# An encoder layer in fp32r halves on one core: conv tiles ahead of v, and the input stage's mean and three roots from column sums on whole tiles

## The chip, the cores and the metric

One core of a Trainium2 chip runs the whole layer. The metric is the device time of one execution in microseconds; it is the median of three runs.

## The reference

One layer of a hybrid encoder, batch 1, 512 tokens (a grid of 8 rows by 64), width 2048, fp32. What matters of it:

```python
xn = rms_norm(x, attn_norm_g[l])
proj = xn @ w_in[l]                          # 2048 -> 5120
u_val, u_gate, q, k, v = split(proj)         # 1024 columns each
h = depthwise_conv(u_val * sigmoid(u_gate), dw_w, dw_b)      # width 31
y_conv = silu(layer_norm(h, ln_g, ln_b))     # over the 1024 channels
y_na = neighborhood_attention(q, k, v, rpb)  # 16 heads of 64, window 8 x 16
mixed = concat(rms_norm(y_conv, conv_out_g), rms_norm(y_na, na_out_g))
x = x + mixed @ w_out[l]                     # 2048 -> 2048
...                                          # norm, gated MLP (5632) with a conv of width 3, norm
```

So the input stage has, over the channels of each token, one mean and one root for the LayerNorm (named `rln`), one root for the conv group's norm (`ra`) and one for the attention group's (`rna`).

## The kernel before

Activations lie transposed: channels on the 128 partitions, 512 tokens along the free axis, so a tile is 128x512. An fp32 product is made of three fp32r products: every weight chunk is loaded raw (SP queue), ScalarE copies it to fp32r (`whi`, L129) and VectorE forms the rest (`wlo`, L130). There are four buffers of each, and `weights()` makes three chunks ahead of the one in use. Nine raw buffers are shared with the conv tiles' accumulators `y` and the attention's bias tables. A *unit* below is one chunk of weights against eight chunks of the input: 16 matmuls with `whi` (L146 and L147) and 8 with `wlo` (L149).

`ORDER` (L63) writes the tiles of the input projection out by hand: `a` is a pair of conv tiles (gate and value, four units), `V` half of v (eight chunks, L396), `q` one attention pair's q and k (four units). Each `a` puts the 31 taps of its depthwise conv into a list; each chunk that is made takes up to `TAPS` = 4 of them, which run on VectorE (L462, L464). The order of VectorE's and ScalarE's queues is chosen by the framework's scheduler when the program is built, from priorities and from "issue after" marks; each engine then runs its queue in order.

Other work hangs on `tick`, which is called behind every unit and moves two generators on by one step, first the attention, then `group_a`:

- The attention takes a pair of heads at a time (pairs 0 to 7): behind one tick come the values of the pair before (L585, `po`) and this pair's scores (L539, `sc`), then the softmax (VectorE L549 to L555, ScalarE L554 and L557). Three ticks later, or four for the pairs in `LATER` = (5, 6), the probabilities are turned on TensorE (L565, `trp`) and copied by ScalarE (L574, `pt`). The values of that pair follow one tick after.
- `group_a` starts when all taps are done: sum of the eight conv tiles (L477, L479), column sums of it on TensorE (L482), the mean (L484), subtraction and squares (L487, L220, L221), the root `rln`, then for each tile the product with it (L494), silu (L495), the split into `mah` and `mal` (L211, L212), squares again (L220, L221), and after `RA_AFTER` ticks the root `ra`.

A root is made in `rsqrt_steps` and `root_steps`: four fp32 matmuls with one column each (L261, eight rows of the trace) bring the sums of squares onto the tokens' partitions; seven operations on 128x4 form the inverse root; it is spread on two diagonal tiles `dg` (eight products of 128x128, L248); one tick later two matmuls with ones (L252) broadcast it to all partitions, and ScalarE copies it (L254). PSUM banks of the projections (`psm`) are three in rotation; `stat()` has one bank that it shares with the values.

The output projection's first half (`out_half(ma, read_a)`, L146 to L149 with names `po` and `mah`) runs while the last attention pairs are still under way; `read_a` holds its results in their banks until `ra` is there (L673, L674). The second half, and the MLP behind it (L800, L939), are not touched.

Of the kernel before, what the change touches and what calls it, by code (L numbers as in the profile page):

```python
# [10 lines left out]
F32 = mybir.dt.float32  # L11
F32R = mybir.dt.float32r
AF = mybir.ActivationFunctionType
ALU = mybir.AluOpType
AX = mybir.AxisListType

P = 128
# [3 lines left out]
CONV = 1024  # L21
HEADS = 16
DH = 64
NA = 1024
# [4 lines left out]
EPS = 1e-6  # L29
# [5 lines left out]
U = 8  # L35
# [18 lines left out]
TAPS = 4  # L54
# [5 lines left out]
Q = D // 2 // S  # L60
TAIL = 4
ROW = 2048
ORDER = "aaaaaVVqaqaqaqqqqq"  # L63
LATER = (5, 6)
RA_AFTER = 5

# [11 lines left out]
def layer(ctx: ExitStack, tc: tile.TileContext, xT, xg, xn, xw, w_0, w_in, w_v, w_out, w_up, w_down, par, tab, g3, out):  # L78
    nc = tc.nc
# [8 lines left out]
    @contextmanager  # L88
    def shifted(by):

        at = tc.cur_priority
        tc.cur_priority = max(at + by, 0)
        yield
        tc.cur_priority = at + (tc.cur_priority - max(at + by, 0))

    def t2(name, dt=F32):
        return tp.tile([P, S], dt, tag="t2k", name=name)

    def t4(shape, name):

        return wpool.tile(shape, F32, tag="raw", name=name, bufs=NR)
# [4 lines left out]
    def pc(name, i):  # L106
        o = POFF[name] + i
        return prm[:, o:o + 1]

    ones_r = consts.tile([P, P], F32R, name="ones")  # L110
    ones = ones_r.bitcast(F32)
# [3 lines left out]
    ps = psm.tile([P, S], F32, tag="mm", name="warm")  # L115
# [5 lines left out]
    def raw_unit(src, n):  # L121
        raw = t4([P, U * P], "raw")
        return raw, nc.sync.dma_start(raw[:, :n], src)

    def parts(raw, n):
        hi = wpool.tile([P, U * P], F32R, tag="whi", name="whi", bufs=NW)
        lo = wpool.tile([P, U * P], F32R, tag="wlo", name="wlo", bufs=NW)
        with tc.issue_after(copies.pop().ins) if copies else nullcontext():
            i = nc.scalar.activation(hi[:, :n], raw[:, :n], AF.Copy)  # L129
        j = nc.vector.tensor_sub(lo[:, :n], raw[:, :n], hi[:, :n].bitcast(F32))  # L130
        with tc.issue_after(j.ins), shifted(600):
            for _ in range(min(len(taps), TAPS)):
                taps.pop(0)()
        return hi, lo, i, j

    def unit(src, n):

        return parts(raw_unit(src, n)[0], n)[:2]

    tight, taps, copies = [], [], []  # L140

# [26 lines left out]
    plan, made = [], []  # L168
# [39 lines left out]
    def split(src, g, name):  # L208

        h, l = t2(name + "h", F32R), t2(name + "l", F32R)  # L210
        nc.scalar.activation(h, src, AF.Copy, scale=g)  # L211
        nc.vector.scalar_tensor_tensor(l, src, g, h.bitcast(F32), op0=ALU.mult, op1=ALU.subtract)  # L212
        return h, l

    def sum_sq(acc, src, first, to=slice(0, S)):
        if first:
            nc.scalar.activation(acc, src, AF.Square)
        else:
            q = t2("sq")[:, to]
            nc.scalar.activation(q, src, AF.Square)  # L220
            nc.vector.tensor_add(acc, acc, q)  # L221

    def stat():
        if where:
            return psa.tile([P, S], F32, tag="tr", name="st", bufs=2)
        return psa.tile([P, S], F32, tag="po", name="st")
# [3 lines left out]
    def root_steps(sums, n, name, keep=None):  # L230

        v, r, y = (sm.tile([P, S // P], F32, tag="rs" + c, name="rs" + c) for c in "vry")
        h = sm.tile([P, S // P], F32R, tag="rsh", name="rsh")
        nc.vector.tensor_scalar(v, sums, 1.0 / n, EPS, op0=ALU.mult, op1=ALU.add)
        nc.scalar.activation(r, v, AF.Sqrt)
        nc.vector.tensor_mul(y, r, r)
        nc.vector.tensor_add(y, y, v)
        nc.vector.reciprocal(y, y)
        nc.vector.scalar_tensor_tensor(y, y, 2.0, r, op0=ALU.mult, op1=ALU.mult)
        nc.vector.tensor_copy(h, y)  # L240
        nc.vector.tensor_sub(v, y, h.bitcast(F32))
        if keep is not None:
            nc.vector.tensor_copy(keep, y)

        dg = [t2("dg", F32R) for _ in range(2)]
        for d, x in zip(dg, (h.bitcast(F32), v)):
            for i in range(S // P):
                nc.vector.tensor_scalar(d[:, i * P:(i + 1) * P], ident, x[:, i:i + 1], None, op0=ALU.mult)  # L248
        yield
        ps = stat()  # L250
        for i in range(2):
            nc.tensor.matmul(ps, ones_r, dg[i], start=i == 0, stop=i == 1)  # L252
        res = t2(name)
        nc.scalar.activation(res, ps, AF.Copy)  # L254
        return res

    def rsqrt_steps(acc, n, name):

        ps = stat()
        for i in range(S // P):  # L260
            nc.tensor.matmul(ps[:, i:i + 1], acc[:, i * P:(i + 1) * P], ones[:, 0:1], start=True, stop=True)  # L261
        return (yield from root_steps(ps[:, :S // P], n, name))


    xs, x1 = [], []
    pin = tc.keep_in_program_order

# [7 lines left out]
    def piece(k0, k1):  # L275
        n = 3 * (k1 - k0) * P
        raw, i = raw_unit(w_0[:, 3 * k0 * P:3 * k1 * P], n)
        pin(i)
        w = parts(raw, n)
        for i in w[2:]:  # L280
            pin(i)
        pieces.append((k0, k1, [w[0]], w[1]))
# [10 lines left out]
    for k in range(ROWS):  # L293
        n = 3 * P
# [3 lines left out]
        x, raw, lo = both[:, :S], both[:, S:S + n], t2("wel", F32R)[:, :n]  # L298
# [4 lines left out]
        else:  # L303
            his = [t2("weh", F32R)[:, :P], t2("weh", F32R)[:, P:n]]
            h, l = t2("xh", F32R), t2("xl", F32R)
# [22 lines left out]
    for u in range(2):  # L328
        raw, i = raw_unit(w_in[1, :, u * U * P:(u + 1) * U * P], U * P)
# [5 lines left out]
    for i in range(6):  # L335
        plan.append(lambda i=i: parts(early[i - 4], U * P)[:2] if i > 3 else None)
    a_, q_, v_ = iter(range(NC_)), iter(range(NP_)), iter(range(2))
    for step in ORDER:
        if step == "V":
            half = next(v_)  # L340
            for u in range(KD // 2):
                plan.append(lambda half=half, u=u: unit(w_v[half, u], U * P))
            continue
        i = next(a_ if step == "a" else q_)
        for n in ((NC_ + i, i) if step == "a" else (2 * NC_ + j * NP_ + i for j in range(2))):
            for u in range(KD // U):
                plan.append(lambda n=n, u=u: unit(w_in[n, :, u * U * P:(u + 1) * U * P], U * P))
    del plan[6:14]
    for half in range(2):
        for d in range(KD):  # L350
            plan.append(lambda half=half, d=d: unit(w_out[half, d], U * P))
# [118 lines left out]
    ma, ra = [], []  # L470

    def group_a():
        yield
        while taps:
            yield
        acc = t2("acc")
        nc.vector.tensor_add(acc, ys[0], ys[1])  # L477
        for i in range(2, NC_):
            nc.vector.tensor_add(acc, acc, ys[i])  # L479
        yield  # L480
        ps = stat()
        nc.tensor.matmul(ps, ones, acc, start=True, stop=True)  # L482
        mu = t2("mu")
        nc.vector.tensor_scalar(mu, ps, 1.0 / CONV, None, op0=ALU.mult)  # L484
        acc = t2("acc")
        for i in range(NC_):
            nc.vector.tensor_sub(ys[i], ys[i], mu)  # L487
            sum_sq(acc, ys[i], i == 0)
        yield
        yield  # L490
        r = yield from rsqrt_steps(acc, CONV, "rln")
        acc = t2("acc")
        for i in range(NC_):
            nc.vector.tensor_mul(ys[i], ys[i], r)  # L494
            nc.scalar.activation(ys[i], ys[i], AF.Silu, scale=pc("lng", i), bias=pc("lnb", i))  # L495
            ma.append(split(ys[i], pc("cog", i), "ma"))
        for i in range(NC_):
            sum_sq(acc, ys[i], i == 0)
        for _ in range(RA_AFTER):
            yield  # L500

        ra.append((yield from rsqrt_steps(acc, CONV, "ra")))


    mb, rb = [], []
    acc_na = t2("accna")
# [119 lines left out]
    p, n = -1, 0  # L626
    for step in ORDER:
        if step == "a":
# [34 lines left out]
    wait = []  # L663

    def norm_b():
        rb.append((yield from rsqrt_steps(acc_na, NA, "rna")))

    def read_a(d, ps):
        wait.append((d, ps))
        while ra and wait:  # L670
# [3 lines left out]
            nc.vector.tensor_add(x2[d], x2[d], t)  # L674

    steps.append(norm_b())
    assert len(ma) == NC_
    out_half(ma, read_a)
# [328 lines left out]
    def all_but_one(th, t):  # L1007

        m = sm.tile([P, 1], F32, tag="nm", name="rsm")
        nc.vector.tensor_reduce(m, sq[th][:, t, :2 * Q - 1], axis=AX.X, op=ALU.add)  # L1010
        nc.vector.tensor_scalar(m, m, 1.0 / D, EPS, op0=ALU.mult, op1=ALU.add)
        return m
# [52 lines left out]
    for i in product2(5, primed, True):  # L1065
        with shifted(-100):
            for _ in ready(e3, primed, 0, 0, (i,), True, fused):
                pass
            if i % Q == Q - 2:
                most = all_but_one(0, i // Q)  # L1070
# [78 lines left out]
```

## Time and profile before

| | |
|---|---|
| median of three runs | 1961.36 us (1961.08 to 1961.88) |
| profiled execution | 1961.11 us, its span 1959.3 us |
| TensorE busy | 1944.6 us |
| VectorE busy | 1607.2 us |
| ScalarE busy | 1083.0 us |
| mean granted TensorE clock | 0.997 |

Times in the profile are from one execution. TensorE matmuls are pipelined, so rows overlap the next; a row's idle time is in brackets, with what ended it. L numbers are lines of the kernel before; where a line of the changed kernel is meant, the text says so.

### The profile page before, as it was taken

To read this page: it belongs to the slowest core of one execution; us is meant where nothing else is said; L and a number is where in the kernel's file an instruction comes from. 1 tells how busy PE (TensorE), PEld (TensorE's weight loads), DVE (VectorE), ACT (ScalarE), POOL (GpSimd) and SP (SyncE) were. 2 spreads that over 40 slices of the span, in tenths; PEclk is the share of its full clock that TensorE was granted. 3 is DMA by queue.
4 is the path that set the end of the run, shared out by engine and by line. 5 is a ranking of instruction groups with operands and counts; after the bars stand their busy time and mean duration, and the time that the engine had idled before them with its cause. 6 is when DMAs were issued, how large, how long until landed. Compare 5 with 4: busy or idle time off the path is not lost.

```text
span 1959.3 us, 28088 instructions
## 1 busy us (share of the span) xinstructions
PE 1944.6 (99%) x10359; PEld 1655.9 (85%) x10359; DVE 1607.2 (82%) x2345; ACT 1083.0 (55%) x1721; POOL 225.4 (12%) x310
## 2 busy tenths in 40 slices
PE   9999999999999999999999999999999999999998
PEld 8888888878788888888888888888888888888886
DVE  5987888887558898888888888888889898885764
ACT  7222344458526666666666666666666644554654
POOL 0111111100011111111111111111110300000000
PEclk9999999999999999999999999999999999999999
DMA  9676767767758899999999999999995966666653
GB/s 372 180 195 178 203 179 189 184 175 225 239 157 211 207 261 242 273 245 267 243 268 248 267 249 263 254 257 260 251 260 165 389 234 236 216 216 193 192 201 121
DMA packets 141530, 448.90 MB, mean 229 GB/s; under 512 B 14928, under 2 KB 27216, under 8 KB 139984
## 3 DMA queue, kind: packets, MB, share of 16 engines
q1 hardware_dynamic: 89168, 291.90, 43.2%
q0 software_dynamic: 42624, 148.92, 34.9%
q10 hardware_dynamic: 9600, 6.29, 1.1%
q8 instruction: 81, 1.33, 0.3%
q14 instruction: 57, 0.47, 0.1%
HBM read 428.17 MB, written 111.15 MB: 275 GB/s over the span
## 4 chain that ended last, share of the span: by engine, by line
PE 95%; DVE 2%; ACT 2%; issue 1%; DMA 0%; DVEq 0%
PE pu L800 44%; PE pd L939 21%; PE pj L146 5%; PE pj L147 5%; PE pj L149 4%; PE pv L396 4%; PE po L149 3%; PE po L146 3%; PE po L147 3%; PE pj L434 1%; PE pj L438 1%; DVE wlo L130 1%; DVE acc L221 0%; PE po L585 0%; PE trp L565 0%
## 5 line engine op out<-in xcount | busy, mean ns | idle before, releaser
L129 ACT ACTIVATE whi<-raw 128x1024 fp32r<-128x1024 f32 (+1 forms) x574 | 604.3, 1055 | 566.5 <-PE pj L147 118.1
L130 DVE TENSOR_TENSOR wlo<-raw,whi 128x1024 fp32r<-128x1024 f32 (+1 forms) x574 | 698.9, 1219 | 215.6 <-ACT whi L129 178.0
L800 PE MATMUL pu<-xc,whi 128*128 128x512 f32 x2464 | 593.6, 391 | 0.0
L800 PEld LDWEIGHTS pu<-xc,whi 128*128 128x128 f32 x2464 | 451.3, 188 | 86.7 <-DVE xc L688 0.4
L800 PEld LDWEIGHTS pu<-xc,wlo 128*128 128x128 f32 x2464 | 319.2, 191 | 13.7
L800 PE MATMUL pu<-xc,wlo 128*128 128x256 f32 x2464 | 324.2, 283 | 0.0
L939 PE MATMUL pd<-whi,ho 128*128 128x512 f32 x1232 | 305.1, 389 | 0.1
L939 PEld LDWEIGHTS pd<-whi,ho 128*128 128x128 f32 x1232 | 231.1, 188 | 48.7 <-DVE vl L813 0.5
L146 PE MATMUL pj<-xh,whi 128*128 128x512 f32 x464 | 183.8, 396 | 0.0
L464 DVE SCALAR_TENSOR_TENSOR y<-ch,prm,y 128x500 f32<-128x500 f32 (+14 forms) x240 | 177.4, 742 | 5.8
L147 PE MATMUL pj<-xl,whi 128*128 128x512 f32 x464 | 181.7, 392 | 0.0
L939 PE MATMUL pd<-wlo,ho 128*128 128x512 f32 x616 | 165.1, 389 | 0.0
L939 PEld LDWEIGHTS pd<-wlo,ho 128*128 128x128 f32 x616 | 115.6, 188 | 24.0
L809 ACT ACTIVATE pu<-pu 128x512 f32<-128x512 f32 x132 | 76.5, 580 | 92.9 <-PE pu L800 92.8
L749 POOL DMA_DIRECT2D raw<-in_w_up x88 | 78.1, 887 | 354.8 <-DVE wlo L130 195.5
L203 POOL DMA_DIRECT2D ws<-in_w_down x88 | 79.4, 902 | 309.0 <-DMA ws<-in_w_down 114.1
L149 PE MATMUL pj<-xh,wlo 128*128 128x512 f32 x464 | 114.7, 389 | 0.0
L146 PEld LDWEIGHTS pj<-xh,whi 128*128 128x128 f32 x464 | 88.0, 190 | 19.9 <-issue 1.9
L147 PEld LDWEIGHTS pj<-xl,whi 128*128 128x128 f32 x464 | 87.9, 189 | 18.1 <-issue 0.2
L149 PEld LDWEIGHTS pj<-xh,wlo 128*128 128x128 f32 x464 | 87.1, 188 | 18.1
L200 POOL DMA_DIRECT2D ws<-ws x44 | 23.1, 526 | 310.7 <-PE pu L800 84.1
L200 POOL DMA_DIRECT2D ws<-in_w_down x44 | 23.2, 528 | 308.5 <-PE pj L149 127.2
(203 smaller groups left out, 2110.2 us busy)
## 6 DMA issues: line engine op xcount, KB each, us to landing
raw<-in_w_up SPq DMA_DIRECT2D x220, 512.0 KB, 5.9
ws<-in_w_down POOLq DMA_DIRECT2D x132, 512.0 KB, 6.1
raw<-in_w_up POOLq DMA_DIRECT2D x88, 512.0 KB, 7.5
raw<-ws SPq DMA_DIRECT2D x88, 512.0 KB, 3.6
raw<-in_w_down SPq DMA_DIRECT2D x66, 512.0 KB, 4.4
raw<-in_w_in SPq DMA_DIRECT2D x58, 512.0 KB, 5.4
ws<-ws POOLq DMA_DIRECT2D x44, 512.0 KB, 5.8
raw<-in_w_out SPq DMA_DIRECT2D x32, 512.0 KB, 5.6
```

What stands on the lines that cost most here:

```text
L129: i = nc.scalar.activation(hi[:, :n], raw[:, :n], AF.Copy)
L130: j = nc.vector.tensor_sub(lo[:, :n], raw[:, :n], hi[:, :n].bitcast(F32))
L146: nc.tensor.matmul(ps, hi, mh, start=first and k == 0, stop=False)
L147: nc.tensor.matmul(ps, hi, ml, start=False, stop=False)
L149: i = nc.tensor.matmul(ps, lo[:, wk * P:(wk + 1) * P], mh, start=False, stop=last and k == len(ws) - 1)
L203: nc.gpsimd.dma_start(wsum[c][k], w_down[k, {1: A21, 2: A11, 4: A11, 6: A12}[c]], accum_op=ALU.add, max_dma_last_dim=ROW)
L396: m = nc.tensor.matmul(banks[c], xs[2 * u + k][x][:, c * P:(c + 1) * P], w[l][:, k * S:(k + 1) * S], start=u == x == l == k == 0, stop=las ...
L464: nc.vector.scalar_tensor_tensor(y[:, a:b], h[:, a + j - PAD:b + j - PAD], prm[:, o:o + 1], y[:, a:b], op0=ALU.mult, op1=ALU.add)
L749: nc.gpsimd.dma_start(a[c], w_up[f, q2], accum_op=ALU.add)
L800: i = nc.tensor.matmul(ps[:, :n], part[:, k * P:(k + 1) * P], comb[c][k][:, :n], start=j == 0 and not more, stop=j == 2 * U - 1, skip_grou ...
L809: nc.scalar.activation(to, ps, AF.Copy)
L939: m = nc.tensor.matmul(ps[i], h[:, o + t * P:o + (t + 1) * P], w[:, d], start=start and not more and kind == 0 and j == 0, stop=stop and k ...
```

## The change

The order of tiles has six conv pairs ahead of v instead of five, the seventh and eighth come before and after the first q, and the other seven q follow without a break. While v is made, five taps are taken per chunk instead of four. The column sums for the mean are made of two fp32r halves instead of fp32. The three roots `rln`, `ra` and `rna` no longer go over 128x4 and diagonals: the sums of squares are split in two halves, two matmuls with ones give the column sums on all partitions at once, and the inverse root is formed there on 128x512 tiles. In `group_a` the number of ticks between the steps changes with it. The first root (`rstd1`) and the MLP's (`rstd2`) stay as they were.

```diff
-ORDER = "aaaaaVVqaqaqaqqqqq"
+ORDER = "aaaaaaVVaqaqqqqqqq"
...
-    def parts(raw, n):
+    def parts(raw, n, most=TAPS):
...
-            for _ in range(min(len(taps), TAPS)):
+            for _ in range(min(len(taps), most)):
                 taps.pop(0)()
...
+    def halved(src):
+
+        h, l = t2("ah", F32R), t2("al", F32R)
+        nc.scalar.activation(h, src, AF.Copy)
+        nc.vector.tensor_sub(l, src, h.bitcast(F32))
+        return h, l
+
+    def column_sums(two):
+
+        ps = stat()
+        for i in range(2):
+            nc.tensor.matmul(ps, ones_r, two[i], start=i == 0, stop=i == 1)
+        return ps
+
+    def roots_of_sums(acc, n, name, wait=1):
+
+        two = halved(acc)
+        for _ in range(wait):
+            yield
+        ps = column_sums(two)
+        v, r, y = t2("v"), t2("r"), t2(name)
+        nc.vector.tensor_scalar(v, ps, 1.0 / n, EPS, op0=ALU.mult, op1=ALU.add)
+        nc.scalar.activation(r, v, AF.Sqrt)
+        nc.scalar.activation(y, r, AF.Square)
+        nc.vector.tensor_add(y, y, v)
+        nc.vector.reciprocal(y, y)
+        nc.vector.scalar_tensor_tensor(y, y, 2.0, r, op0=ALU.mult, op1=ALU.mult)
+        return y
...
-                plan.append(lambda half=half, u=u: unit(w_v[half, u], U * P))
+                plan.append(lambda half=half, u=u: unit(w_v[half, u], U * P, TAPS + 1))
...
             nc.vector.tensor_add(acc, acc, ys[i])
+        two = halved(acc)
         yield
-        ps = stat()
-        nc.tensor.matmul(ps, ones, acc, start=True, stop=True)
+        yield
+        ps = column_sums(two)
...
         yield
         yield
-        r = yield from rsqrt_steps(acc, CONV, "rln")
+        yield
+        r = yield from roots_of_sums(acc, CONV, "rln")
...
-        ra.append((yield from rsqrt_steps(acc, CONV, "ra")))
+        ra.append((yield from roots_of_sums(acc, CONV, "ra")))
...
-        rb.append((yield from rsqrt_steps(acc_na, NA, "rna")))
+        rb.append((yield from roots_of_sums(acc_na, NA, "rna")))
```

More of the change, by code (lines that the diff above doesn't have):

```diff
@@ L131, in parts, with unit @@
         with tc.issue_after(j.ins), shifted(600):
-            for _ in range(min(len(taps), TAPS)):
+            for _ in range(min(len(taps), most)):
                 taps.pop(0)()
         return hi, lo, i, j
-    def unit(src, n):
-        return parts(raw_unit(src, n)[0], n)[:2]
+    def unit(src, n, most=TAPS):
+        return parts(raw_unit(src, n)[0], n, most)[:2]
     tight, taps, copies = [], [], []
```

## The prediction

> **What bounds the kernel now.** I read the page's busy times and its chain first, then the waits of TensorE, then its timeline wherever those waits lie.
>
> ```profile
> span 1959.3 us, 28088 instructions
> PE 1944.6 (99%) x10359; PEld 1655.9 (85%) x10359; DVE 1607.2 (82%) x2345; ACT 1083.0 (55%) x1721; POOL 225.4 (12%) x310
> PE 95%; DVE 2%; ACT 2%; issue 1%; DMA 0%; DVEq 0%
> ```
>
> TensorE (PE) is 99% busy and carries 95% of the chain. VectorE (DVE) is next at 82%, but nothing of it counts unless PE waits for it. So the change can act in two ways only: in PE's own instructions, and in the waits of PE. The waits of PE and of its weight loads:
>
> ```profile
> PE st L261 <- DVE acc L221: 3.5, 1, 3.5
> PE st L252 <- DVE dg L248: 1.8, 2, 1.6
> PEld po L585 <- ACT pt L574: 0.4, 1, 0.4
> ```
>
> Two of them are waits for root statistics. The third is small, but it says that one attention pair's products with v (po) came just as its probabilities (pt) were copied. Now PE's timeline around the roots. The columns are start, duration, engine, line, operation, tiles, count, and in brackets the idle time before it.
>
> ```profile
> 402.68 1.44 PE L585 MATMUL po<-pt,v 64*64 64x64 f32 x48
> 403.95 1.53 PE L539 MATMUL sc<-k,q 64*64 64x192 f32 x36
> 410.99 1.02 PE L482 MATMUL st<-acc,ones 128*128 128x512 f32 x2
> ...
> 422.77 1.48 PE L565 MATMUL trp<-ident,s 128*128 128x128 f32 x12
> 428.68 1.87 PE L261 MATMUL st<-ones,acc 128*128 128x1 f32 x8 [3.49 <-DVE acc L221]
> 430.98 0.63 PE L147 MATMUL pj<-xl,whi 128*128 128x512 f32 x1
> 431.40 0.63 PE L146 MATMUL pj<-xh,whi 128*128 128x512 f32 x1
> 437.17 1.44 PE L585 MATMUL po<-pt,v 64*64 64x64 f32 x48
> ...
> 482.90 0.95 PE L261 MATMUL st<-ones,acc 128*128 128x1 f32 x8
> 487.48 1.98 PE L149 MATMUL po<-mah,wlo 128*128 128x512 f32 x8
> 493.80 0.47 PE L252 MATMUL st<-dg,ones 128*128 128x512 f32 x1 [1.63 <-DVE dg L248]
> 495.27 1.98 PE L149 MATMUL po<-mah,wlo 128*128 128x512 f32 x8
> 497.09 1.48 PE L565 MATMUL trp<-ident,s 128*128 128x128 f32 x12
> 503.95 1.44 PE L585 MATMUL po<-pt,v 64*64 64x64 f32 x48
> 505.22 1.53 PE L539 MATMUL sc<-k,q 64*64 64x192 f32 x36
> 510.45 1.98 PE L149 MATMUL po<-mah,wlo 128*128 128x512 f32 x8
> 515.89 1.98 PE L149 MATMUL po<-mah,wlo 128*128 128x512 f32 x8
> 523.15 1.48 PE L565 MATMUL trp<-ident,s 128*128 128x128 f32 x12
> 535.01 1.05 PE L261 MATMUL st<-ones,accna 128*128 128x1 f32 x8
> ```
>
> One unit (16 matmuls with the high weights, 8 with the low) lasts 515.89 - 510.45 = 5.44 us. A turn (trp) and a unit last 503.95 - 497.09 = 6.86. The same stretch at 422.77 lasts 437.17 - 422.77 = 14.40, that is 7.54 too much: the eight small statistics, 3.49 us of waiting, and then matmuls 0.42 us apart, where a unit of 24 in 5.44 us has them 0.23 apart.
>
> **The change, what it removes.** The root of the LayerNorm (rln) loses those 7.54 us. Its two broadcast matmuls are replaced by two column-sum matmuls of the same shape (about 0.47 a pair), which cancels; so it does in all three roots. The root ra loses 0.95 of small matmuls and the dg wait: 495.27 - 487.48 = 7.79 is a unit, a pair and 1.88 more. The root rna loses 1.05 and next to no wait. The mean's fp32 matmul, 1.02, becomes a pair of 0.47: 0.55 less. Sum: 7.54 + 0.95 + 1.88 + 1.05 + 0.55 = 12.0 us, all on PE's path.
>
> **What it adds.** Prices, by form (mean ns is the second number behind the bar), from 230 to 560 us and for the 128x1 row from 1880 us on:
>
> ```profile
> L130 DVE TENSOR_TENSOR wlo<-raw,whi 128x1024 fp32r<-128x1024 f32 x52 | 63.1, 1221 | 21.1 <-ACT whi L129 8.2 <-PE po L149 6.8 <-PE pj L149 6.1
> L221 DVE TENSOR_TENSOR acc<-acc,sq 128x512 f32<-128x512 f32 x14 | 9.6, 687 | 0.5
> L212 DVE SCALAR_TENSOR_TENSOR mal<-y,prm,mah 128x512 fp32r<-128x512 f32 x8 | 6.0, 749 | 2.7 <-ACT mah L211 2.7
> L220 ACT ACTIVATE sq<-y 128x512 f32<-128x512 f32 x14 | 7.6, 617 | 0.0
> L554 ACT ACT_TABLE_LOAD x7 | 9.0, 1283 | 0.1
> L1021 DVE RECIPROCAL rsv<-rsv 128x1 f32<-128x1 f32 x4 | 0.7, 162 | 0.1
> L555 DVE RECIPROCAL su<-su 128x2 f32<-128x2 f32 x32 | 5.1, 162 | 19.9 <-ACT s L554 19.6
> L238 DVE RECIPROCAL rsy<-rsy 128x4 f32<-128x4 f32 x3 | 0.5, 179 | 0.1
> ```
>
> The whole-tile reciprocal (128x512) is in no row. If it streamed as the additions do it would take 0.69 us. From 2 to 4 elements the rows rise by 17 ns, 8.5 ns for each; carried on to 512 that is 162 + 510 x 8.5 = 4.5 us. From 1 to 2 they don't rise, so the slope is rough. I take 4.5, since a row of the same operation is nearer than one of another, and keep 0.69 to 4.5 for the range. The Trainium skill (VectorE: DVE Perf Modes, section "First, the fixed hardware budget") says that a reciprocal is an iterative divide with a repeat count of 8, a rule that speaks against a root on whole tiles. At one element in 8 cycles of the 0.96 GHz that its specifications give, my estimate from that page is 4.3 us, and by it the sum below would be 0.2 us less.
>
> Now the place. In the built program the mean's sums come four units earlier, rln's and ra's about one earlier, and rna's stay where they were. Moving rln matters most, for what stands behind it on ScalarE (ACT). Before, silu, splits and squares of the eight conv tiles stand between the scores of attention pair 5 and the copies of its turned probabilities; pair 5 is one of those in LATER, with four ticks before its turn. In the changed program the ACT queue, in its own line numbers and without the silus and splits in the middle, is
>
> ```
> L585 Activation s,su<-s,nm (last exp of pair 4)
> L268 Activation ah<-acc 128x512
> L588 Activation s<-s,su 128x192 x2
> L129 Activation whi<-raw 128x1024 x2
> L287 LoadActFuncSet, L287 r<-v, L288 rln<-r
> L526 LoadActFuncSet, L526 y<-y,prm x8 with L211 mah<-y,prm x8
> L217 acc<-y, L220 sq<-y x7
> L605 pt<-trp 128x384 x4 (pair 4)
> ```
>
> and PE's is: values of pair 3, scores of pair 4, two units, column sums of rln, a unit, turn of pair 4, a unit, values of pair 4. So values of pair 4 wait for pt, and pt stands behind the whole block. How long the block takes, the trace of before shows:
>
> ```profile
> 450.50 4.91 DVE L494 TENSOR_TENSOR y<-y,rln 128x512 f32<-128x512 f32 x8 [0.31 <-ACT rln L254]
> ...
> 453.42 1.53 ACT L495 ACTIVATE y<-y,prm 128x512 f32<-128x512 f32 x2
> 462.77 1.05 ACT L129 ACTIVATE whi<-raw 128x1024 fp32r<-128x1024 f32 x1
> 470.06 1.59 ACT L574 ACTIVATE pt<-trp 128x384 f32<-128x384 f32 x4
> ...
> 471.87 1.44 PE L585 MATMUL po<-pt,v 64*64 64x64 f32 x48
> ...
> 489.43 2.00 ACT L129 ACTIVATE whi<-raw 128x1024 fp32r<-128x1024 f32 x2
> 517.09 0.17 DVE L555 RECIPROCAL su<-su 128x2 f32<-128x2 f32 x1 [1.40 <-ACT s L554]
> ```
>
> From the first silu to the end of pt: 471.65 - 453.42 = 18.2, less two whi copies among them of 1.0 each (the last row but one), which the new order has ahead of the block: 16.2 us. PE's values came at 471.87, right behind: before, the block just fitted.
>
> In the clock of before's trace, PE reaches the values of pair 3 at 402.68 in before. Up to there the changed order holds the same units and as many turns, scores and values; it adds the mean's pair, so 403.15, and scores of pair 4 at 404.42. A clean softmax takes 517.09 + 0.17 - 505.22 = 12.04 us from the start of its scores to its last reciprocal: 416.5. Then al (0.69): 417.2. PE stands at the column sums after 523.15 - 503.95 - 5.44 = 13.76, at 416.9: a wait of 0.3, and they end at 417.6. ACT: the last copies of s, 0.8, then two whi, 2.0: 419.3, while its table load is hidden. DVE: the second wlo until 420.6, v (priced as an addition, 0.69) until 421.3. ACT's root and square, 0.62 each: 422.5 (a root of this size is in no row; the square is nearest). DVE: addition 0.69, reciprocal 4.5, product 0.75, first y 0.69: 429.1. Block, 16.2: 445.3. Durations of DVE rows overlap the next by 0.07 (eight in 4.91), about 0.4 here: 444.9. PE is there at 417.6 + 5.44 + 6.86 = 429.9. **The new wait is 15.0 us.** With a reciprocal of 0.69 it is 11.2.
>
> After 3.49 us of idling the matmuls ran at half pace: of the 7.54 us, 7.54 - 3.49 - 0.95 = 3.1 were that. I add 3.1 once, between 1.5 (half of it) and 5 (values and scores, 2.8 us of small matmuls, stretched too). The Trainium skill (TensorE: Matmul & The Clock Gate, section "What's actually happening") has the half clock come after an idle window of about 3.4 us and go after as long a busy one. By that rule the penalty is 1.7 us or a little over, my estimate from it, and the sum 1.4 lower; this trace's 3.1 differs, so the trace's is used.
>
> Behind that, ra. Its v, root and square stand behind pair 6's softmax, and its four vector steps have three wlo between them, so the first oa product, which must empty the bank for the fourth output tile, is late. From the scores of pair 6: last exp 11.8, copies 0.8, table 1.28, root 0.62, whi 1.05, square 0.62, addition 0.69, three wlo 3.7, reciprocal 4.5, product 0.75, oa 0.69: 26.5, less 0.5 of overlap. PE gets there after one unit with the scores (7.04 to the end of the one at 510.45), a pair, three units and a turn: 25.2. Wait: 0.8 (0 to 2.5). The root rna has six units until it is used, so its longer steps cost nothing. The fifth tap in v's units is hidden: a tap is an operation like mal, and 1.22 + 5 x 0.75 = 5.0 stays under the 5.44 of a unit. So is the mean's split, which stands units ahead of its matmul; without that cover it would cost 0.7. The new tile order moves weight loads of one size past each other on the SP queue and leaves POOL's sums, one to every second unit, where they were; with DMA at 0% of the chain I cost this at nothing. If the weights came late, PE would wait for whi, and no such wait is on its list.
>
> Added: 0.3 + 15.0 + 3.1 + 0.8 = 19.2. Less 12.0: +7.2. Against the profiled execution of 1961.11 us (0.25 under the median of the runs): **1968.3 us**.
>
> **The rivals.**
> - Faster. Nothing waits for the block: pair 4's copies end before PE needs them at 429.9. Then all that is left of the additions is the 0.3 and some of ra's 0.8, say 0.7, and the time is 1961.1 - 12.0 + 0.7 = 1949.8. For it: before hid the same block to within a fraction. Against it: the hiding took four ticks and five units, and now three ticks and two units are left. It decides if the block starts 15 us sooner, while it can't start before the column sums at 417. Chance 0.06.
> - The reciprocal streams (0.69). The wait is 11.2, ra is in time: 1961.1 - 12.0 + 0.3 + 11.2 + 3.1 = 1963.7. The 128x4 row is against it, the 128x1 row for it. Chance 0.14.
> - Still slower. Softmax of pair 4 or the taps behind it are late by a few us, as DVE is at 82%, and the cold stretch takes 5 us, ra 2.5: 1961.1 - 12.0 + 0.3 + 18 + 5 + 2.5 = 1974.9. Chance 0.10.
> - My forecast has 0.70.
>
> **How the numbers follow.** A difference under 0.2%, 3.9 us, is about what can't be told from none. The forecast's own range, with the cold stretch and ra at their ends, is 1966 to 1973. The range for 8 in 10 reaches down over most of the streaming reciprocal and up into the last rival: 1961.5 to 1973.5. Streaming ends in the "same" band (up to 1965.3), the first rival is faster, the others slower: 0.06, 0.14, 0.80.
>
> **What would show it.** In the changed profile: one wait of PE at po for pt, of 11 to 16 us, near 430; matmuls at half pace behind it; no wait for dg, and none over 1 us at the column sums; RECIPROCAL rows of 128x512 at 4 to 4.5 us; fewer table loads on ACT, without effect. If po doesn't wait, or the block's first silu starts before 424, the forecast is wrong.

## The result and the profile after

The changed kernel takes 1965.49 us (median of 13 runs, 1964.9 to 1966.24), the kernel before 1961.08 (13 runs, 1960.26 to 1961.88). The ratio is 1.0022 with a 95% interval of 1.0015 to 1.0029: 4.4 us slower, where 7.2 were forecast. The profiled execution took 1964.9 us with a span of 1963.1, which is 3.8 over the span before. It is the shortest of the 13 runs: the granted clock is 0.996 in it and in the next three, and 0.994 or 0.995 in the other nine, which took 1965.4 us or more; what lowers the clock in those, no trace shows. Sums of single waits below are made against the spans, and results of experiments are compared by their medians.

From the page of the changed kernel, the span, the busy times and the chain's shares by engine:

```profile
span 1963.1 us, 28018 instructions
PE 1939.8 (99%) x10335; PEld 1653.3 (84%) x10335; DVE 1616.0 (82%) x2316; ACT 1080.1 (55%) x1720; POOL 225.9 (12%) x310
PE 97%; ACT 1%; DVE 1%; issue 0%; ACTq 0%
```

TensorE's busy time fell from 1944.6 to 1939.8 us, by 4.8 (matmuls at a lower clock count with their longer time, so this isn't the removed work alone). Yet the span grew by 3.8, so TensorE's idle time grew by 8.6. TensorE's waits in the changed kernel, all of them (the second row is the start of the program), and the longest of its weight loads:

```profile
PE po L616 <- ACT pt L605: 14.0, 1, 14.0
PE warm L117 <- DVE ones L112: 1.1, 1, 1.1
...
PEld po L616 <- ACT pt L605: 14.4, 1, 14.4
```

The waits for root statistics (3.5 and 1.8 us) are gone, and one new wait of 14.0 us stands in their place: the products with v of attention pair 4 wait for the copies of its turned probabilities. TensorE's timeline around it, in the changed kernel's line numbers (L276 is the column sums, L596 the turn, L616 the values, L570 the scores):

```profile
416.61 0.39 PE L276 MATMUL st<-ah,ones 128*128 128x512 f32 x1
416.83 0.39 PE L276 MATMUL st<-al,ones 128*128 128x512 f32 x1
...
420.71 1.98 PE L149 MATMUL pj<-xh,wlo 128*128 128x512 f32 x8
422.53 1.48 PE L596 MATMUL trp<-ident,s 128*128 128x128 f32 x12
...
427.49 1.97 PE L149 MATMUL pj<-xh,wlo 128*128 128x512 f32 x8
443.44 2.62 PE L616 MATMUL po<-pt,v 64*64 64x64 f32 x48 [13.97 <-ACT pt L605]
445.84 2.67 PE L570 MATMUL sc<-k,q 64*64 64x192 f32 x36
...
452.21 1.98 PE L149 MATMUL pj<-xh,wlo 128*128 128x512 f32 x8
```

The column sums run without a gap. TensorE is ready for the values at 443.44 - 13.97 = 429.47, and the probabilities were turned by 424.0. What it waits for stands on ScalarE. ScalarE's timeline of the same stretch:

```profile
421.50 1.28 ACT L526 ACT_TABLE_LOAD   x1
427.08 1.52 ACT L526 ACTIVATE y<-y,prm 128x512 f32<-128x512 f32 x2 [4.30 <-DVE y L525]
...
436.41 1.32 ACT L211 ACTIVATE mah<-y,prm 128x512 fp32r<-128x512 f32 x2
437.64 0.61 ACT L217 ACTIVATE acc<-y 128x512 f32<-128x512 f32 x1
438.16 3.73 ACT L220 ACTIVATE sq<-y 128x512 f32<-128x512 f32 x7
441.80 1.59 ACT L605 ACTIVATE pt<-trp 128x384 f32<-128x384 f32 x4
```

The eight silus, eight splits and eight squares go first, and ScalarE idles 4.30 us ahead of them, waiting for VectorE's first product with the root, while the four copies that TensorE needs stand behind the block. VectorE's timeline says what the 4.30 us are:

```profile
415.55 0.69 DVE L269 TENSOR_TENSOR al<-acc,ah 128x512 fp32r<-128x512 f32 x1 [0.35 <-ACT ah L268]
417.19 2.36 DVE L130 TENSOR_TENSOR wlo<-raw,whi 128x1024 fp32r<-128x1024 f32 x2 [0.95 <-ACT whi L129]
419.46 0.68 DVE L286 TENSOR_SCALAR v<-st 128x512 f32<-128x512 f32 x1
421.51 0.69 DVE L289 TENSOR_TENSOR rln<-rln,v 128x512 f32<-128x512 f32 x1 [1.36 <-ACT rln L288]
422.24 3.35 DVE L290 RECIPROCAL rln<-rln 128x512 f32<-128x512 f32 x1
425.63 0.69 DVE L291 SCALAR_TENSOR_TENSOR rln<-rln,r 128x512 f32<-128x512 f32 x1
426.35 4.90 DVE L525 TENSOR_TENSOR y<-y,rln 128x512 f32<-128x512 f32 x8
```

The last three steps of the inverse root (an addition, the reciprocal and a product) and the first product with the root, one after the other, take from 421.51 to about 427.0, and the first silu starts at 427.08.

Then the half clock: behind the wait TensorE is granted only half of its clock for a while. TensorE in stretches of the changed kernel (window, its length, busy time and count of PE, PEld, DVE, ACT and POOL, then the granted clock, DMA share and GB/s):

```profile
416.00:429.00 13.00, 13.00 (x65) 10.92 (x64) 10.58 (x12) 7.85 (x10) 2.31 (x3) 1.00 0.60 161
429.00:443.00 14.00, 0.47 (x3) 0.04 (x1) 11.76 (x18) 14.00 (x26) 0.00 (x0) 0.70 0.40 98
443.00:450.00 7.00, 6.56 (x91) 5.78 (x92) 6.00 (x9) 4.12 (x7) 0.00 (x0) 0.63 0.81 267
450.00:460.00 10.00, 10.00 (x46) 8.27 (x45) 5.49 (x14) 8.83 (x27) 0.64 (x2) 1.00 0.51 176
```

Behind the wait the clock is 0.63 on average for 7 us. In steps of 0.25 us the same trace has it at 0.50 from 434.5 to 448.2, so for the first 4.8 us behind the wait, and at 1.00 ahead of that and after. Values, scores and the first sixteen matmuls of a unit take 452.21 - 443.44 = 8.77 us; before, without a wait, the same took 510.45 - 503.95 = 6.50. The half clock costs 2.3 us, about half of those 4.8.

So 14.0 + 2.3 = 16.3 us were added. Less the forecast's 12.0 of removed terms that is +4.3, and the spans show +3.8: the removed terms were worth about 0.5 more than they were put at.

### The profile page after: what moved, and what is told of

Same layout as the page of the kernel before. It is cut to its first block, busy times and chain, and to the rows that moved or that the text cites. A ratio compares the mean times of both kernels' runs of the same rounds, so it can differ in the third digit from the quotient of the medians.

```text
span 1963.1 us, 28018 instructions
## 1 busy us (share of the span) xinstructions
PE 1939.8 (99%) x10335; PEld 1653.3 (84%) x10335; DVE 1616.0 (82%) x2316; ACT 1080.1 (55%) x1720; POOL 225.9 (12%) x310
## 4 chain that ended last, share of the span: by engine, by line
PE 97%; ACT 1%; DVE 1%; issue 0%; ACTq 0%
PE pu L831 44%; PE pd L970 21%; PE pj L146 5%; PE pj L147 5%; PE pj L149 5%; PE pv L425 4%; PE po L146 3%; PE po L147 3%; PE po L149 3%; PE pj L463 1%; PE po L616 1%; PE pj L467 1%; PE sc L570 1%; PE trp L596 0%; PE trx L726 0%; ACT y L526 0%
## 5 line engine op out<-in xcount | busy, mean ns | idle before, releaser
L831 PEld LDWEIGHTS pu<-xc,wlo 128*128 128x128 f32 x2464 | 319.2, 191 | 13.7
```

The source lines that it names most:

```text
L831: i = nc.tensor.matmul(ps[:, :n], part[:, k * P:(k + 1) * P], comb[c][k][:, :n], start=j == 0 and not more, stop=j == 2 * U - 1, skip_grou ...
```

## The experiments

The theory was that the time lies in ScalarE's queue: what stands ahead of pair 4's copies, and for how long, sets the new wait, and the half clock follows. The rivals were that the roots' longer steps on VectorE are the cost by themselves, that the order of tiles alone does it, and that the root `ra` or VectorE's load takes over once the wait is gone. Ratios are to the kernel before, whose median beside these runs was 1961.14, 1961.28 and 1960.6 us in the three groups (the first four, the next four, the last two).

**A cheap step for the reciprocal.** In the changed kernel, for `rln` only; the reciprocal is left out there, so `rln` is no inverse root:

```diff
-        nc.vector.reciprocal(y, y)
+        if name == "rln":
+            nc.vector.tensor_add(y, y, v)
+        else:
+            nc.vector.reciprocal(y, y)
```

> The changed kernel with the reciprocal of rln replaced by one more addition of the same tile (so rln is not the inverse root here). Theory: the values of attention pair 4 wait for ScalarE's block behind rln, and every step of rln is on that path one for one. The reciprocal took 3.35 us, an addition takes 0.69, so the wait of 14.0 us falls by 2.7 to 11.3, and the time by 2.7 to about 1962.8. Rival (the wait is set by something else, the bank of the fifth k or the weights): wait and time stay, 1965.5.

Measured: 1963.19 us (1961.88 to 1964.07), ratio 1.0011 (1.0002 to 1.002). TensorE's waits in this kernel:

```profile
PE po L619 <- ACT pt L608: 11.3, 1, 11.3
```

The wait fell by 2.7 us, which is the reciprocal's 3.35 less an addition's 0.69. The wait follows the steps of this root one for one. The time fell by 2.3 between the medians.

**The squares later.** The eight squares for `ra` are moved two ticks behind the splits, and `RA_AFTER` is two less, so that `ra` comes when it came:

```diff
-RA_AFTER = 5
+RA_AFTER = 3
...
             ma.append(split(ys[i], pc("cog", i), "ma"))
+        for _ in range(2):
+            yield
         for i in range(NC_):
             sum_sq(acc, ys[i], i == 0)
```

> The changed kernel, with the squares for ra issued two ticks later, behind the copies of pair 4's turned probabilities (and ra's own ticks fewer by two, so that ra stays where it is). Theory: the squares, 437.64 to 441.89 on ScalarE, no longer stand ahead of the copies; the wait falls by 4.2 to about 9.8 us and the time by 4.2 to about 1961.3. Rival (the wait has another cause): 1965.5 as before. Second rival: the squares now crowd pair 5's softmax and make its turn late: time gains less than 3 us.

Measured: 1961.16 us (1960.44 to 1962.02), ratio 1.0 (0.9991 to 1.0009), as expected. TensorE's wait:

```profile
PE po L618 <- ACT pt L607: 9.8, 1, 9.8
```

From the first square to the copies, ScalarE's timeline above has 441.80 - 437.64 = 4.16 us; the wait is 4.2 shorter. The place in the queue is what costs, not the work: no operation was taken out.

**The whole block later.** The same two ticks, but between the root and its first use:

```diff
-RA_AFTER = 5
+RA_AFTER = 3
...
         r = yield from roots_of_sums(acc, CONV, "rln")
+        for _ in range(2):
+            yield
         acc = t2("acc")
```

> The changed kernel, with two ticks between the root rln and the block that uses it (products, silu, splits, squares), so that pair 4's copies go ahead of the block. Theory: no wait of TensorE is left at pair 4's values; the wait of 14.0 and the 2.3 us of half clock behind it both go, pair 5's copies end near 456 and its values are not due before 460: time about 1949.2, 12 us under the kernel before. Rival: the block only moves the wait to pair 5, whose exponentials stand among it: a wait of 5 us or more there, time 1955 or above.

Measured: 1949.29 us (1948.87 to 1949.63), ratio 0.994 (0.9927 to 0.9952). This is 16.2 us below the changed kernel and 11.8 below the kernel before; it is the shortest time of all. Its span is 1947.5 us, and its waits on TensorE are

```profile
PE warm L117 <- DVE ones L112: 1.1, 1, 1.1
PE pj L463 <- DVE g L340: 0.4, 1, 0.4
```

ScalarE's timeline of this kernel, and then TensorE's values of pairs 4 and 5:

```profile
423.69 1.64 ACT L607 ACTIVATE pt<-trp 128x384 f32<-128x384 f32 x4 [1.91 <-PE trp L598]
...
430.37 2.23 ACT L528 ACTIVATE y<-y,prm 128x512 f32<-128x512 f32 x3
...
453.63 3.74 ACT L220 ACTIVATE sq<-y 128x512 f32<-128x512 f32 x7
457.28 1.58 ACT L607 ACTIVATE pt<-trp 128x384 f32<-128x384 f32 x4
```

```profile
429.70 1.44 PE L618 MATMUL po<-pt,v 64*64 64x64 f32 x48
...
461.20 1.44 PE L618 MATMUL po<-pt,v 64*64 64x64 f32 x48
```

The copies of pair 4 now run ahead of the silus, at 423.69, and TensorE has its values at 429.70 with nothing before them. The splits and squares of the block lie in front of the copies of pair 5, which end at 458.86, 2.3 us before TensorE comes. The wait and the half clock, 13.97 + 2.3, less the 0.4 of the one wait that is new, are 15.9 us; the spans differ by 15.6 and the medians by 16.2. It also answers what would be late next: nothing over 0.4 us.

**The order alone.** The kernel before, with only the new order of tiles:

```diff
-ORDER = "aaaaaVVqaqaqaqqqqq"
+ORDER = "aaaaaaVVaqaqqqqqqq"
```

> The kernel before with the new order of tiles alone; old roots, four taps throughout. Theory: the old root reaches TensorE later (its broadcast stands behind pair 4's turn), so the block stays behind pair 4's copies and no wait arises there; the statistics of rln are in time, since the taps end earlier, so the 3.5 us wait and the half clock behind it go (6.6 us together): about 1954.5. Rival: the order itself is what costs (attention pairs every four units crowd VectorE and ScalarE): 1961 or above.

Measured: 1963.28 us (1961.16 to 1964.62), ratio 1.0007 (0.9998 to 1.0016). The expectation missed by 9 us. TensorE's waits in the profiled run, which was the shortest of the eleven:

```profile
PE st L482 <- DVE acc L479: 3.0, 1, 3.0
PE pj L146 <- DVE ao L594: 2.7, 1, 2.7
...
PEld pj L146 <- issue: 5.0, 9, 3.1
```

The wait at `rln`'s statistics did go, and in this trace the half clock with it (granted clock 0.999). In their place the mean's sums come too late for TensorE (3.0), and one later projection waits too (2.7; the 3.1 of the weight loads is the same stop). In six of the eleven runs, the median among them, the granted clock is 0.996 or 0.997 and the time 1963.28 us or more; a half clock behind one of these waits would fit that, but no trace of those runs shows it. The changed kernel has five taps to a unit in v and a second tick ahead of the mean's column sums, and no such wait; which of the two does it was not tried. The order is worth nothing by itself.

**The roots alone.** The changed kernel with the old order, four taps in v, one tick ahead of the mean's sums and two ahead of the root:

```diff
-ORDER = "aaaaaaVVaqaqqqqqqq"
+ORDER = "aaaaaVVqaqaqaqqqqq"
...
-                plan.append(lambda half=half, u=u: unit(w_v[half, u], U * P, TAPS + 1))
+                plan.append(lambda half=half, u=u: unit(w_v[half, u], U * P))
...
         two = halved(acc)
         yield
-        yield
         ps = column_sums(two)
...
-        yield
         yield
         yield
```

> The old order of tiles and four taps throughout, with the mean and the three roots from column sums on whole tiles; the ticks in front of the mean and of rln are the old ones (one and two). Theory: here the block behind rln stands after pair 4's copies, as before, so no wait arises at pair 4's values, and the 3.5 us wait with its half clock goes, since the split sums get a tick of their own; VectorE's longer steps come when it has least time to spare, which may leave a wait of 2 to 5 us at pair 5's values or for a wlo: 1950 to 1956. Rival (the roots need the new order, without it the wait for the sums stays): 1961 or above.

Measured: 1965.9 us (1964.62 to 1966.77), ratio 1.0023 (1.0014 to 1.0033). It missed by 10 us or more. TensorE's waits:

```profile
PE po L146 <- DVE oa L702: 7.1, 1, 7.1
PE po L614 <- ACT pt L603: 5.0, 1, 5.0
```

Both are steps that the prediction had: `ra` late for the bank of the fourth output tile (put at 0.8 for the new order), and copies of probabilities behind the block, here those of pair 5. With the old order the longer roots come too late; with the new order and the old ticks the mean does. The parts need each other, and their effects don't add.

**Three reciprocals for one.** The version with the block later, with two more reciprocals in `rln` (the value stays the same), 6.7 us of VectorE:

```diff
         nc.vector.reciprocal(y, y)
+        if name == "rln":
+            nc.vector.reciprocal(y, y)
+            nc.vector.reciprocal(y, y)
```

> The kernel with the block two ticks later, with two more reciprocals of rln, 6.7 us of VectorE (an even number of inversions is added, so rln keeps its value). Theory: with the block behind pair 4's copies nothing on TensorE waits for rln's steps at once, so 6.7 us more cost at most 1.5 us, by pair 5's copies: 1949.3 to 1950.8. Rival (rln's steps are on the path in any place): 1956.

Measured: 1956.51 us (1956.19 to 1957.62), ratio 0.9976 (0.9966 to 0.9986), 7.2 us over the version without them. At most 1.5 were expected; the number is the rival's, but not its reason. TensorE's wait, and the matmul that had it:

```profile
PE pj L146 <- ACT whi L129: 5.3, 1, 5.3
```

```profile
461.60 0.79 PE L146 MATMUL pj<-xh,whi 128*128 128x512 f32 x1 [5.28 <-ACT whi L129]
```

It isn't the probabilities that are late here but the weight copies `whi`, which the longer block pushes back on ScalarE (in this kernel the block also fell behind the exponentials of pair 5). So 6.7 us are more than the block can be delayed by, and the first to be late is something else in ScalarE's queue. As the order of that queue changed as well, the 7.2 are no price of the reciprocals alone. In the trace, which is of the longest of the nine runs, they are the wait of 5.3 and a half clock behind it, 5.8 us long.

**The old roots, one after the other.** All from the version with the block later: old steps for `ra` and `rna`; old steps for `rln`; old steps for all three.

```diff
-        ra.append((yield from roots_of_sums(acc, CONV, "ra")))
+        ra.append((yield from rsqrt_steps(acc, CONV, "ra")))
...
-        rb.append((yield from roots_of_sums(acc_na, NA, "rna")))
+        rb.append((yield from rsqrt_steps(acc_na, NA, "rna")))
```

> The kernel with the block two ticks later, with the old roots for ra and rna. Theory, from the terms of the prediction's sum: ra's small matmuls 0.95 and its wait for dg 1.9, rna's small matmuls 1.05: 3.9 us more, 1953.2. If ra's wait for dg was due to its place in the old order, only 2.0 more: 1951.3. Rival (the whole-tile roots gave nothing there): 1949.3.

```diff
-        r = yield from roots_of_sums(acc, CONV, "rln")
+        r = yield from rsqrt_steps(acc, CONV, "rln")
```

> The kernel with the block two ticks later, with the old root for rln. Theory: the sums of squares are ready when the small matmuls come, one unit earlier than the column sums; they cost their 0.94 us and no half clock, 1950.2, unless they come ahead of the sums and wait: then 3 us and the half clock's 2.4 more, up to 1956. Rival (the whole-tile root is what makes the place free): 1956 or above without such a wait at the sums.

Both of these edits together:

> The kernel with the block two ticks later, with the old roots for rln, ra and rna together; the new order, the fifth tap in v's part and the mean from split sums stay. Theory: the two measured parts add up, 2.2 for rln and 5.5 for ra and rna over 1949.3: 1957, so the order, the ticks and the split mean bring 4 us of the 12 and the whole-tile roots 8. Rival (either half of the roots brings the gain by itself, since both removed the same cause): under 1955.

Measured: `ra` and `rna` old 1954.82 us (1954.14 to 1955.67; ratio 0.9968, 0.9955 to 0.998), `rln` old 1951.48 (1950.85 to 1951.54; 0.995, 0.9937 to 0.9962), all old 1953.83 (1953.72 to 1954.18; 0.9964, 0.9952 to 0.9977). The waits of the three, in this order:

```profile
PE st L261 <- DVE acc L221: 2.0, 1, 2.0
...
PE st L252 <- DVE dg L248: 0.2, 1, 0.2
```

```profile
PE st L252 <- DVE dg L248: 1.0, 1, 1.0
```

```profile
PE st L252 <- DVE dg L248: 1.1, 2, 0.9
...
PE st L261 <- DVE acc L221: 0.2, 1, 0.2
```

Over the 1949.29 they cost 5.5, 2.2 and 4.5 us, where 3.9, 0.9 and 7.7 were expected. In the first, a wait of 2.0 for `ra`'s sums came in place of the one of 1.9 for `dg`; in the second, a wait of 1.0 for `dg` came on top. And 5.5 + 2.2 is not 4.5, since with `rln` old as well the wait of 2.0 for `ra`'s sums is nearly gone. With all old roots, the order, the taps, the ticks and the mean's split sums are still worth about 7 us against the kernel before, and the whole-tile roots the other 4.5.

**One more root.** The version with the block later, and the MLP's root on whole tiles as well:

```diff
-        rstd2.append((yield from rsqrt_steps(acc2, D, "rstd2")))
+        rstd2.append((yield from roots_of_sums(acc2, D, "rstd2")))
```

> The kernel with the block two ticks later, with the MLP's root rstd2 from column sums on whole tiles too. Theory: its eight small matmuls (0.94 us) go from TensorE's path, and its longer steps on VectorE are needed only when the first MLP tile is finished: 1948.4. Rival (the 3.4 us reciprocal delays VectorE in its busiest stage, the combinations for the MLP's first products): 1950 or above.

Measured: 1950.34 us (1950.05 to 1950.91), ratio 0.9946 (0.9932 to 0.996), 1.05 us more than without; 0.9 less was expected, and the rival came. TensorE's busy time is 0.5 less (1937.0 against 1937.5), but it has a wait that it didn't have:

```profile
PE pu L833 <- DVE vl L846: 1.9, 1, 1.9
```

The up projection's first banks are emptied by VectorE, which is later here. In its queue the reciprocal (3.35 us at 676.4) stands ahead of the operation that TensorE waits for, `vl`, which starts at 681.71; without the change it starts at 678.98. No run takes the reciprocal alone out.

## Why the prediction was right, and where its sizes were off

**The place and the kind were right.** One wait of TensorE at the values of pair 4, for copies that stand behind the block of silus, splits and squares: forecast for 429.9, come at 429.47. Moving the block away took the wait and the half clock back and nothing else; moving the squares or shortening the root took back just their own length.

By the number alone the forecast couldn't be told from a rival: 1965.49 us lies half a microsecond under the forecast's own range of 1966 to 1973, and nearer to the 1963.7 of the streaming reciprocal than to 1968.3. The trace tells them apart, with a reciprocal of 3.35 us and a wait of 14.0 where that rival has 0.69 and 11.2. The sizes below were nearly all off to the same side, so they didn't cancel.

**The wait was put at 15.0 us and is 14.0.** The block was right: 16.2 forecast, and from the first silu to the end of the copies 443.39 - 427.08 = 16.3. Its end, 443.39, came 1.5 us earlier than the 444.9 worked out. The step that was mis-sized most is the reciprocal: 4.5 by the slope of two short rows, 3.35 measured. By the Trainium skill, VectorE: DVE Perf Modes, section "First, the fixed hardware budget", the prediction's estimate was 4.3; the measurement decides. The other is the start of the chain: `al` was done at 416.24 and not at 417.2, which also took the 0.3 us at the column sums away. Against these 2.1 us stands the 0.4 of overlap that the prediction had taken off, and the block came 0.1 longer. As TensorE itself came 0.4 us sooner, the wait is 1.0 shorter and not 1.5.

**The half clock was put at 3.1 and is 2.3.** The 3.1 was the price of one restart, taken over as that of another. Before, TensorE starts again at 428.68, and its clock in stretches is

```profile
425.00:430.00 5.00, 1.51 (x8) 1.33 (x7) 3.52 (x5) 2.49 (x3) 0.91 (x1) 0.79 0.59 195
430.00:436.00 6.00, 6.00 (x19) 4.85 (x20) 3.79 (x16) 0.76 (x2) 0.00 (x0) 0.60 0.84 198
```

In finer steps it is at 0.50 until 434.7, so for 6.1 us behind the restart, against 4.8 in the changed kernel. Half of each is 3.0 and 2.4, which is the price within 0.1: what counts is how long the half clock lasts behind the restart. Values and scores ran at 2.62 and 2.67 us for 1.44 and 1.53 meanwhile, and the bound of 5 wasn't met. Nor was the 1.7 that the prediction worked out from the Trainium skill (TensorE: Matmul & The Clock Gate, section "What's actually happening"). That estimate takes one busy window of about 3.4 us from the restart on, while the section calls the window free-running; a restart can then fall inside one window and wait for the end of the next, and the 4.8 and 6.1 us here agree with that.

**The root `ra` was put at 0.8 and costs nothing,** as 0 to 2.5 allowed: the shorter reciprocal alone gives back 1.15. With the old order the wait did come, with 7.1 us.

**The removed work was put at 12.0.** With the block later, what is left is 1947.5 against 1959.3, 11.8 between the spans, with a wait of 0.4 among what stays. So the sum of the terms holds to within 0.5; where that half microsecond lies was not followed further, and the terms weren't measured one by one.

Together: 15.0 - 14.0, 3.1 - 2.3, 0.8 and 0.3 are 2.9 us of the additions that did not come, and 7.2 less these is 4.3, against 3.8 between the spans and 4.4 between the medians.

**The edits costed at nothing** were the fifth tap, the mean's split, the weight order, POOL's sums and `rna`'s longer steps. No wait points to any of them in the changed kernel. Of the signs that were named, all came but one: the reciprocals are not 4 to 4.5 us long.

**The rivals.** "Nothing waits" was put at 1949.8, and it fell by its own test: the first silu would have had to start about 15 us sooner. Two ticks of delay reached the same end from the other side, with 1949.29. A streaming reciprocal was put at 1963.7; taking the reciprocal out gave 1963.19, so that rival's price was nearly right and its condition wrong.

## What to carry to other kernels

Here ScalarE ran its queue in order, so a step that was moved earlier took its followers with it: ask of each engine what stands behind the moved block and who waits for that, not whether the block itself is early enough. About 12 us were removed and 16.3 added, because short copies that TensorE needs stood behind 16 us of work that nobody needed yet, and delaying that work by two ticks turned 4.4 us of loss into 11.8 of gain. Parts of such a change are to be tried together as well as apart: the order alone and the roots alone each brought nothing, and both with the right ticks brought 0.6%.

## What was not expected of the hardware

A reciprocal of 128x512 took 3.35 us on VectorE, 6.5 ns for each element of a partition and nearly five times the 0.69 us of an addition of that size; all three in the changed kernel are within 0.01 us. The slope between two short rows had given 8.5 ns. Two of the three rows:

```profile
L290 DVE RECIPROCAL rln<-rln x1: 3353/3353/3353, 422.2 to 422.2; 128x512 f32<-128x512 f32 x1
L290 DVE RECIPROCAL ra<-ra x1: 3347/3347/3347, 495.3 to 495.3; 128x512 f32<-128x512 f32 x1
```

The cost of the half clock did not grow with the wait: 3.1 us behind 3.5 us of waiting (before), 2.5 behind 11.3 (the cheap step for the reciprocal), 2.4 behind 9.8 (the squares later), 2.3 behind 14.0. In these traces the clock is at 0.50 in a single stretch of 6.8, 13.7, 10.2 and 13.7 us, each a multiple of 3.41 to within 0.03. It began 2.7, 2.8, 4.6 and 5.1 us after TensorE fell idle, where it costs nothing yet, and ended 6.1, 5.1, 5.0 and 4.8 us after TensorE started again. Waits of 3.0 and 2.7 us (the order alone) and of 2.0 (`ra` and `rna` old) have no half clock in their traces. So a wait of 3.5 us cost nearly as much in clock as in waiting, and one of 3.0 cost nothing more.
